# A hybrid decoder block on one core: the convolution norm in an early and a late part, and the first chunk's scores with the next four chunks'

## The chip, the core and the metric

The kernel runs on one core of one Trainium2 chip. The core has five engines that each work through their own queue of instructions in order: TensorE (PE, the matmuls, with PEld for its weight loads), VectorE (DVE), ScalarE (ACT), GpSimd (POOL) and SyncE (SP, which here only issues DMAs). They meet through semaphores. The metric is the device time of one execution in microseconds; lower is better.

## The reference

One decoder layer over 16 learned meta tokens and 512 tokens of 1024 channels, all in float32. Cut to what matters here:

```
p = layer_norm(concat(meta, x)) @ w_in          # one combined projection
c = p[:, :1024] * sigmoid(p[:, 1024:2048])      # conformer branch
c = causal_dwconv(c, 31 taps) + b
c = silu(layer_norm(c over channels, g, b)) @ w_conv_out
# RWKV-7 branch, 16 heads of 64, state S per head:
S_t = S_{t-1} diag(decay_t) + (S_{t-1} a_t) b_t^T + v_t k_t^T ;  y_t = S_t r_t
B = group_norm(y) ... @ w_rwkv_out
y = sigmoid(gA) * c + sigmoid(gB) * B
h = layer_norm(ALPHA*h + y @ w_o);  out = layer_norm(ALPHA*h + conv_gated_mlp(h))
```

## The kernel before

Channels lie on the 128 partitions, tokens along the free axis: 528 tokens in two halves of 272 and 256. Every large product is done in three matmuls per 128 channels of contraction (high part times high part, low times high, high times low), so a product of 128 output channels over one half of the tokens is a group of 24 matmuls into one PSUM bank. I call these groups the gemms. Their weights come by DMA (`wr`), ScalarE makes the high part (`wh`, L153) and VectorE the low part (`wl`, L154).

The eight PSUM banks are handed out by four rotating tags: three banks for `gbank` (all gemms of the first stage), two for `xbank` (the chain over chunks), two for `abank` and one for `mbank` (the preparation and small things).

The string SCHEDULE gives the program order of the first stage in steps, one letter and a pair of heads (0 to 7) each. G is `glu`, the conformer's gated product (four gemms). K is `rkv`, the projections k, v and r of a pair of heads (six gemms; r is last). P is `prep`, which turns them into the operands of the recurrence in 9 chunks of 64 tokens. S is `solve`, the triangular solves of a pair, a long run of small dependent VectorE operations, with the steps of a depthwise convolution `conv` of 48 VectorE operations put between them. C is `chain`, the recurrence from chunk to chunk. F is `finish`, A is `gate` (two gemms), T a convolution alone, N the norm of the convolutions, and H (before only) marks where gemms written later in the program are held behind the norm's mean. A priority scheduler then fixes each engine's queue: an instruction that is ready goes in order of its priority (program order, earlier inside `with front()`), and a tile from a rotating pool needs its place in the rotation.

`prep` in order, with the lines of before: two pairs of small products for decay and rate per half (L406, L407, L417, L418; row `ps_a<-lwp,wuh` and so on), tanh on ScalarE, squares summed per token (L454, `ps_m<-e,sq`), a scan on VectorE (L423, `cum`), exponentials, six products on VectorE that make the operands `AR` and `BK` (L434 to L448), the reciprocal norms (`nsc`, L456 to L460), their spread `nsb` transposed on TensorE (L468) and multiplied into `BK` (L470). Then come the bonus term `bv` (L478, L479), the scores of chunk 0, chunks 1 to 4 and chunks 5 to 8 (L490, each part of two heads into two `abank` banks, and L492 that masks them into `Gt`), a scaling of `AR` on ScalarE and transposes of `BK` and `v` (L506, L510).

`conv_norm` (N) loads the eight convolution results from `c_dr`, adds them (`csum`), forms the mean by a product with a matrix of ones (L802), subtracts it, squares on ScalarE and adds (`qsum`), forms the variance (L812), the root and its reciprocal, then scales, applies silu and splits into `zh`, `zl` for the product with `w_conv_out` (its first two weights at L182 to L184). It opens a pool of its own over the memory that the first stage leaves.

Of the kernel before, what the change touches and what calls it, by code (L numbers as in the profile page):

```python
# [11 lines left out]
F32 = mybir.dt.float32  # L12
F32R = mybir.dt.float32r
AF = mybir.ActivationFunctionType
ALU = mybir.AluOpType
# [3 lines left out]
P = 128  # L19
D = 1024  # L20
NK = D // P
SEQ = 512
NMETA = 16
T = SEQ + NMETA
HD = 64
NH = 16
NCH = 9
# [3 lines left out]
KC = 31  # L31
Q0 = 14
NQ = T - Q0
# [13 lines left out]
GW = 132  # L47


SCHEDULE = ("G0 K0 P0 T0 G1 S01 K1 P1 C0 K2 F0 G2 S12 K3 P2 C1 G3 F1 K4 S23 G4 P3 C2 F2 A S34 K5 P4 C3 F3 G5 S4 A "  # L50
            "T5 K6 P5 G6 C4 F4 S56 P6 C5 K7 F5 G7 S67 A A A P7 C6 F6 S7 A A C7 A A N A A A A H A A A F7")


@with_exitstack
def hybrid_block(ctx: ExitStack, tc: tile.TileContext, a, out, dbg=None):
    nc = tc.nc
    V, S, G, TE = nc.vector, nc.scalar, nc.gpsimd, nc.tensor
# [5 lines left out]
    def pool(stack, name, side, **kw):  # L63
        return stack.enter_context(tc.tile_pool(name=name, bufs=1, side=side, reuse_waits="tile", **kw))

    front = tc.high_priority
# [30 lines left out]
    ones_d = cp.tile([P, P], F32, name="ones_d")  # L97
# [9 lines left out]
    cmask = cp.tile([P, P], F32, name="cmask")  # L107
# [56 lines left out]
    def wload(dram, c0, wpool=None, bufs=2):  # L164
        return wsplit(wcols(dram, c0), [P, NK, P], wpool, bufs)

    hold = []

    def gemm(ps, w, xh, xl, sl, nk=NK):
        wh, wl = w  # L170
        for k in range(nk):
            first = TE.matmul(ps, wh[:, k, :], xh(k, sl), start=(k == 0), stop=False)  # L172
            if k == 0 and hold:
                behind(first, hold[-1], "work kept for the norm's waits")
            TE.matmul(ps, wl[:, k, :], xh(k, sl), start=False, stop=False)  # L175
            TE.matmul(ps, wh[:, k, :], xl(k, sl), start=False, stop=(k == nk - 1))  # L176

# [9 lines left out]
    turn, turn_a = cycle((gbank, xbank, gbank, xbank, gbank)), cycle((gbank, abank, gbank, abank, gbank))  # L187
# [21 lines left out]
    sp = pool(ctx_a2, "scan", "left")  # L209
    c_dr = dr.tile([NK, P, NQ], F32, name="c_dr")  # L210
# [38 lines left out]
    with tc.tile_pool(name="start", bufs=1, side="right", reuse_waits="tile") as st:  # L249
# [25 lines left out]
        for i, n in enumerate(names):  # L275
            src = a[n][0].rearrange("(r q) n -> r (q n)", q=2) if n == "r_k" else vec(n)
# [50 lines left out]
        for r_ in wr_:  # L327
            hi, lo, first = wparts(r_, [P, NK, P], wp)
# [9 lines left out]
        c0 = 43  # L338
        for i, n in ((1, 112), (2, 128), (3, 120), (4, 88), (5, 44)):
# [15 lines left out]
                    in1=taps[:, :, 1, :], op=ALU.add)  # L355
# [20 lines left out]
    ra = pool(ctx_a1, "proj", "right")  # L376
# [10 lines left out]
    def prep(p, r, k, v):  # L387
# [15 lines left out]
        for hf, (t0, t1) in enumerate(HALF):  # L403
            n = t1 - t0
# [3 lines left out]
            if hf == 0:  # L408
# [21 lines left out]
        AR = sp.tile([P, NCH, P], F32, name="AR", bufs=2)  # L430
        BK = ra.tile([P, NCH, P], F32, name="BK", bufs=1)
# [7 lines left out]
                               in1=Ei[:, :, 1:65], op0=ALU.mult, op1=ALU.mult)  # L439
        sq = ra.tile([P, 640], F32, name="sq", tag="tmp", bufs=2)[:, 0:OFF + T]  # L440
# [10 lines left out]
        pm = mbank()  # L451
# [12 lines left out]
        for g0, g1, c0, c1 in ((0, 3, 0, 5), (3, 5, 5, NCH)):  # L464
            pt = abank()
            for i in range(g0, g1):
# [4 lines left out]
                            in1=pt[:, 0:64 * (c1 - c0)].rearrange("p (c t) -> p c t", t=64), op=ALU.mult)  # L471


        bv = sp.tile([P, NQ], F32, name="bv", bufs=2)
        for t0, t1 in QH:
            pt = abank()
            n = t1 - t0
            TE.matmul(pt[:, :n], bones, rk[:, OFF + t0:OFF + t1], start=True, stop=True)  # L478
            V.tensor_tensor(out=bv[:, t0 - Q0:t1 - Q0], in0=pt[:, :n], in1=v[:, 64 + OFF + t0:64 + OFF + t1],  # L479
                            op=ALU.mult)  # L480


        Gt = sp.tile([P, 2, NCH, GW], F32, name="Gt", bufs=2)
        G.memset(Gt.rearrange("p h c (two x) -> p (h c two) x", two=2)[:, :, 64:66], 0.0)
        for c0, c1 in ((0, 1), (1, 5), (5, 9)):
            pts = [abank(), abank()]
            for c in range(c0, c1):
                for h in range(2):
                    o = pts[h][:, P * (c - c0):P * (c - c0 + 1)]
                    TE.matmul(o, BK[64 * h:64 * h + 64, c, :], AR[64 * h:64 * h + 64, c, :], start=True, stop=True)  # L490
            for h in range(2):
                V.tensor_tensor(out=Gt[:, h, c0:c1, :].rearrange("p c (two x) -> p c two x", two=2)[:, :, :, 0:64],  # L492
                                in0=pts[h][:, 0:P * (c1 - c0)].rearrange("p (c two t) -> p c two t", two=2, t=64),
                                in1=cmask.rearrange("p (two t) -> p two t", two=2).unsqueeze(1).broadcast_to(
                                    [P, c1 - c0, 2, 64]), op=ALU.mult)

        for c in range(1, NCH):
            S.activation(out=AR[:, c, :], in_=AR[:, c, :], func=AF.Copy, scale=lc[:, c - 1:c])
# [269 lines left out]
    def gate(j):  # L768
        w = wload(w_in, C_GA + P * j)
        gt = sp.tile([P, NQ], F32, name="gt", bufs=2)  # L770
        for t0, t1 in QH:
            pt = gbank()
            n = t1 - t0
            gemm(pt[:, :n], w, hh, hl, slice(t0, t1))
            with front():
                S.activation(out=gt[:, t0 - Q0:t1 - Q0], in_=pt[:, :n], func=AF.Tanh, scale=0.5,
                             bias=dcol(D_HBG, j))
        nc.sync.dma_start(out=g_dr[j], in_=gt)
# [3 lines left out]
    ctx_b1 = ExitStack()  # L782


    def conv_norm():
        rb = pool(ctx_b1, "conv", "right")
        zt = lambda dt, name: rb.tile([P, NQ], dt, name=name, tag="z", bufs=17)
        cs = []
        csum = rb.tile([P, NQ], F32, name="csum")
        for j in range(NK):  # L790
            c_t = zt(F32, "c_t")
            nc.sync.dma_start(out=c_t, in_=c_dr[j])
            cs.append(c_t)
            if j == 1:
                V.tensor_tensor(out=csum, in0=cs[0], in1=cs[1], op=ALU.add)
            elif j > 1:
                V.tensor_tensor(out=csum, in0=csum, in1=c_t, op=ALU.add)
        qsum = rb.tile([P, NQ], F32, name="qsum")
        rstd = rb.tile([P, NQ], F32, name="rstd")
        for sl, n in qsl:  # L800
            pm = abank()
            mean = TE.matmul(pm[:, :n], ones_d, csum[:, sl], start=True, stop=True)  # L802
            for j in range(NK):
                V.tensor_tensor(out=cs[j][:, sl], in0=cs[j][:, sl], in1=pm[:, :n], op=ALU.subtract)
        for j in range(NK):
            sq = qsum if j == 0 else zt(F32, "csq")
            S.activation(out=sq, in_=cs[j], func=AF.Square)
            if j > 0:
                V.tensor_tensor(out=qsum, in0=qsum, in1=sq, op=ALU.add)
        for sl, n in qsl:  # L810
            pm = abank()
            TE.matmul(pm[:, :n], ones_d, qsum[:, sl], start=True, stop=True)  # L812
            S.activation(out=rstd[:, sl], in_=pm[:, :n], func=AF.Sqrt, bias=eps_ln)
            V.reciprocal(out=rstd[:, sl], in_=rstd[:, sl])
        zh, zl = [], []
        for j in range(NK):
            V.tensor_tensor(out=cs[j], in0=cs[j], in1=rstd, op=ALU.mult)
            S.activation(out=cs[j], in_=cs[j], func=AF.Silu, scale=par("conv_ln_g", j), bias=par("conv_ln_b", j))
            zh.append(zt(F32R, "zh"))
            zl.append(zt(F32R, "zl"))  # L820
            split(zh[j], zl[j], cs[j])
        return rb, zh, zl, mean

    raw, prs, solved, ys, cpads = {}, {}, {}, {}, {}
    gates = list(range(16))
    for step in SCHEDULE.split():
        what, p, q = step[0], int(step[1:2] or 0), int(step[2:] or -1)
        if what == "K":
            raw[p] = rkv(p)
        elif what == "P":  # L830
            prs[p] = prep(p, *raw.pop(p))
        elif what == "S":
            solved[p] = solve(prs[p], conv(q, cpads.pop(q)) if q >= 0 else ())
        elif what == "C":
            with front():
                merge(prs[p], *solved[p])
                ys[p] = chain(prs[p])
        elif what == "F":
            finish(prs[p], ys.pop(p))
        elif what == "G":  # L840
            cpads[p] = glu(p)
        elif what == "T":
            with back():
                for _ in conv(p, cpads.pop(p)):
                    pass
        elif what == "A":
            gate(gates.pop(0))
        elif what == "N":
            ctx_a1.close()
            rb, zh, zl, mean = conv_norm()  # L850
        elif what == "H":
            hold.append(mean)
    hold.clear()
    for j in range(NK):
        ga = rb.tile([P, NQ], F32, name="ga", bufs=2)
        nc.sync.dma_start(out=ga, in_=g_dr[j])
# [23 lines left out]
    op = pool(ctx_o, "rout", "left")  # L880
# [119 lines left out]
    for j in range(2, NF):  # L1000
        c = j - 2
# [80 lines left out]
```

## Time and profile before

| | before |
|---|---|
| median of 3 runs | 1181.84 us (1171.94 to 1184.82) |
| profiled execution | 1175.08 us, its span 1173.0 us |
| TensorE busy | 1121.2 us, 96% of the span |
| VectorE busy | 862.9 us, 74% |
| ScalarE busy | 567.5 us, 48% |
| mean granted TensorE clock | 0.989 |

The busy time of TensorE is that of pipelined matmuls, so a full share does not say that it runs at its peak; its gaps are what is read here. The median of the runs is 0.6% above the profiled execution. The execution has 2.1 us around its span.

### The profile page before, as it was taken

To read this page: it belongs to the slowest core of one execution; us is meant where nothing else is said; L and a number is where in the kernel's file an instruction comes from. 1 tells how busy PE (TensorE), PEld (TensorE's weight loads), DVE (VectorE), ACT (ScalarE), POOL (GpSimd) and SP (SyncE) were. 2 spreads that over 40 slices of the span, in tenths; PEclk is the share of its full clock that TensorE was granted. 3 is DMA by queue.
4 is the path that set the end of the run, shared out by engine and by line. 5 is a ranking of instruction groups with operands and counts; after the bars stand their busy time and mean duration, and the time that the engine had idled before them with its cause. 6 is when DMAs were issued, how large, how long until landed. Compare 5 with 4: busy or idle time off the path is not lost.

```text
span 1173.0 us, 22681 instructions
## 1 busy us (share of the span) xinstructions
PE 1121.2 (96%) x8718; PEld 1056.2 (90%) x8718; DVE 862.9 (74%) x2179; ACT 567.5 (48%) x1214; POOL 83.6 (7%) x242
## 2 busy tenths in 40 slices
PE   5999999999999999999987999999999999999997
PEld 4998989899898989989887999998999999998885
DVE  6598998889899998976586366697876666662228
ACT  5644456637556565665577433355434343441120
POOL 7001011101101110101000000000000000000000
PEclk9999999999999999999988999999999999999999
DMA  5333341333414143354432476531332323333321
GB/s 163 84 93 92 87 97 50 87 77 91 101 56 109 42 103 79 85 125 106 140 100 65 139 227 203 158 88 54 109 109 73 108 73 109 89 123 113 102 78 72
DMA packets 202438, 118.99 MB, mean 101 GB/s; under 512 B 50036, under 2 KB 186397, under 8 KB 202331
## 3 DMA queue, kind: packets, MB, share of 16 engines
q1 hardware_dynamic: 182992, 113.81, 34.6%
q10 hardware_dynamic: 17515, 3.17, 1.5%
q8 instruction: 68, 1.11, 0.4%
q0 software_dynamic: 1824, 0.57, 0.3%
q14 instruction: 39, 0.32, 0.1%
HBM read 102.24 MB, written 15.28 MB: 100 GB/s over the span
## 4 chain that ended last, share of the span: by engine, by line
PE 65%; DVE 7%; DMA 4%; ACT 3%; issue 2%; DVEq 0%; ACTq 0%; POOL 0%; SPq 0%; POOLq 0%
PE ps_x L624 7%; PE ps_g L175 6%; PE ps_g L176 6%; PE ps_g L172 6%; PE ps_g L182 4%; PE ps_g L183 4%; PE ps_g L184 4%; PE psf L1027 3%; PE psf L1026 3%; PE psf L1028 3%; PE ps_x L182 3%; PE ps_x L183 3%; PE ps_x L184 3%; ACT wh L153 1%; PE ps_a L490 1%
## 5 line engine op out<-in xcount | busy, mean ns | idle before, releaser
L172 PE MATMUL ps_g<-hhi,wh 128*128 128x256 f32 (+2 forms) x944 | 278.9, 296 | 2.6 <-DVE v L227 1.7
L175 PE MATMUL ps_g<-hhi,wl 128*128 128x256 f32 (+2 forms) x944 | 278.6, 295 | 0.0
L176 PE MATMUL ps_g<-hlo,wh 128*128 128x256 f32 (+2 forms) x944 | 278.0, 295 | 0.0
L154 DVE TENSOR_TENSOR wl<-wr,wh 128x1024 fp32r<-128x1024 f32 x151 | 182.6, 1220 | 96.8 <-ACT wh L153 96.5
L153 ACT CAST wh<-wr 128x1024 fp32r<-128x1024 f32 x151 | 158.2, 1049 | 128.9 <-PE psf L1027 73.4
L172 PEld LDWEIGHTS ps_g<-hhi,wh 128*128 128x128 f32 x944 | 180.5, 191 | 5.2 <-DVE v L227 2.2
L175 PEld LDWEIGHTS ps_g<-hhi,wl 128*128 128x128 f32 x944 | 180.1, 191 | 2.6 <-issue 0.6
L176 PEld LDWEIGHTS ps_g<-hlo,wh 128*128 128x128 f32 x944 | 180.3, 191 | 1.4 <-issue 0.4
L182 PE MATMUL ps_g<-hhi,wh 128*128 128x256 f32 (+1 forms) x424 | 120.0, 283 | 0.0
L183 PE MATMUL ps_g<-hhi,wl 128*128 128x256 f32 (+1 forms) x424 | 119.2, 281 | 0.4 <-DVE wl L154 0.4
L184 PE MATMUL ps_g<-hlo,wh 128*128 128x256 f32 (+1 forms) x424 | 118.9, 281 | 0.0
L762 DVE SCALAR_TENSOR_TENSOR cev<-cd,drv,cev 128x257 f32<-128x257 f32 x216 | 99.1, 478 | 0.1
L182 PE MATMUL ps_x<-hhi,wh 128*128 128x256 f32 (+1 forms) x280 | 79.0, 282 | 1.7 <-ACT hhi L138 1.7
L183 PEld LDWEIGHTS ps_g<-hhi,wl 128*128 128x128 f32 x424 | 79.7, 188 | 0.7 <-DVE wl L154 0.7
L182 PEld LDWEIGHTS ps_g<-hhi,wh 128*128 128x128 f32 x424 | 79.7, 188 | 0.3 <-ACT wh L153 0.2
L184 PEld LDWEIGHTS ps_g<-hlo,wh 128*128 128x128 f32 x424 | 79.8, 188 | 0.0
L183 PE MATMUL ps_x<-hhi,wl 128*128 128x256 f32 (+1 forms) x280 | 78.6, 281 | 0.0
L184 PE MATMUL ps_x<-hlo,wh 128*128 128x256 f32 (+1 forms) x280 | 78.5, 280 | 0.0
L624 PE MATMUL ps_x<-UV,Gt 128*66 128x64 f32 (+1 forms) x576 | 70.7, 245 | 3.4 <-DMA Gt<-dT 2.6
L624 PEld LDWEIGHTS ps_x<-UV,Gt 128*66 128x66 f32 (+1 forms) x576 | 64.9, 166 | 5.1 <-DMA Gt<-dT 2.8
L1027 PE MATMUL psf<-wh,hidl 128*128 128x512 f32 x176 | 69.3, 394 | 0.0
L1026 PE MATMUL psf<-wh,hidh 128*128 128x512 f32 x176 | 69.0, 392 | 0.0
(371 smaller groups left out, 2542.6 us busy)
## 6 DMA issues: line engine op xcount, KB each, us to landing
wr<-in_w_in_dram SPq DMA_DIRECT2D x59, 512.0 KB, 4.3
wr<-in_ffn_up_dram SPq DMA_DIRECT2D x44, 512.0 KB, 4.0
wr<-in_ffn_down_dram SPq DMA_DIRECT2D x22, 512.0 KB, 3.6
wr<-in_w_o_dram SPq DMA_DIRECT2D x10, 512.0 KB, 4.9
g_dr<-gt SPq DMA_DIRECT2D x16, 257.0 KB, 2.9
L<-dA SPq DMA_DIRECT2D x32, 128.0 KB, 4.0
wr<-in_w_conv_out_dram SPq DMA_DIRECT2D x8, 512.0 KB, 4.3
wr<-in_w_rwkv_out_dram SPq DMA_DIRECT2D x8, 512.0 KB, 6.2
```

Of the source, the lines that this page charges most:

```text
L153: first = S.copy(out=hi, in_=raw)
L154: V.tensor_tensor(out=lo, in0=raw, in1=hi.bitcast(F32), op=ALU.subtract)
L172: first = TE.matmul(ps, wh[:, k, :], xh(k, sl), start=(k == 0), stop=False)
L175: TE.matmul(ps, wl[:, k, :], xh(k, sl), start=False, stop=False)
L176: TE.matmul(ps, wh[:, k, :], xl(k, sl), start=False, stop=(k == nk - 1))
L182: TE.matmul(ps, wh[:, k, :], xh(k, sl), start=(k == 0), stop=False)
L183: TE.matmul(ps, wl[:, k, :], xh(k, sl), start=False, stop=False)
L184: TE.matmul(ps, wh[:, k, :], xl(k, sl), start=False, stop=(k == nk - 1))
L624: mm = lambda o, l, r, start: TE.matmul(o, l, r, start=start, stop=True, skip_group_check=True)
L762: yield V.scalar_tensor_tensor(out=yp[:, b, :] if lasttap else ev[:, b, :], in0=d[:, i:i + NM], scalar=dcol(D_HCW, 8 * (2 * i + b) + j), i ...
L1026: TE.matmul(acc[t][d], hidh[:, k, ts], wd[k][0][:, ds], start=(k == 0), stop=False)
L1027: TE.matmul(acc[t][d], hidl[:, k, ts], wd[k][0][:, ds], start=False, stop=False)
```

## The change

Two edits. First, `prep` takes the banks of the first chunk's scores from `gbank` and `mbank` (two `abank` banks before), issues the scores of chunk 0 and of chunks 1 to 4 one behind the other at raised priority with the two heads in a fixed alternation, masks both parts after that, then does chunks 5 to 8; the bonus term `bv` moves behind the scores. Second, the norm is cut in two. A new step M, `conv_sums`, works in tiles of the convolutions' own memory (`cpad`, three buffers, `cacc`, `cev`): it loads the results one by one, adds them, takes the mean, loads them a second time, subtracts the mean, stores the centred values to a new `cc_dr`, squares and sums them and makes the reciprocal root. The late part N only loads `cc_dr`, scales, applies silu and splits. The step H and its `hold` go. In SCHEDULE, P7 moves ahead of the three gates that stood before it, and M stands behind P7.

```diff
-            "T5 K6 P5 G6 C4 F4 S56 P6 C5 K7 F5 G7 S67 A A A P7 C6 F6 S7 A A C7 A A N A A A A H A A A F7")
+            "T5 K6 P5 G6 C4 F4 S56 P6 C5 K7 F5 G7 S67 P7 M C6 A A A F6 S7 A A C7 A A N A A A A A A A F7")
...
-            if k == 0 and hold:
-                behind(first, hold[-1], "work kept for the norm's waits")
...
+        parts = ((0, 1), (1, 5), (5, 9))
+        score_banks = {}
+        for i, (c0, c1) in enumerate(parts):
+            pts = score_banks[i] = [gbank(), mbank()] if i == 0 else [abank(), abank()]
+            with front():
+                for c in range(c0, c1):
+                    for h in range(2):
+                        o = pts[h][:, P * (c - c0):P * (c - c0 + 1)]
+                        score = TE.matmul(o, BK[64 * h:64 * h + 64, c, :], AR[64 * h:64 * h + 64, c, :], start=True,
+                                          stop=True)
+                        if h == 0 and c > c0:
+                            behind(score, other, "the heads in turn")
+                        other = score
+            if i == 0:
+                continue
+            for i_, h in ((0, 0), (0, 1), (1, 0), (1, 1)) if i == 1 else ((2, 0), (2, 1)):
+                ... (the masking into Gt, as before)
...
-        for c0, c1 in ((0, 1), (1, 5), (5, 9)):
-            pts = [abank(), abank()]
-            for c in range(c0, c1):
-                for h in range(2):
-                    o = pts[h][:, P * (c - c0):P * (c - c0 + 1)]
-                    TE.matmul(o, BK[64 * h:64 * h + 64, c, :], AR[64 * h:64 * h + 64, c, :], start=True, stop=True)
...
+    def conv_tile(src=None):
+        c_t = ra.tile([P, 2, (KC - 1 + T) // 2], F32, name="cpad", bufs=3).rearrange("p two n -> p (two n)")[:, 0:NQ]
+        if src is not None:
+            nc.sync.dma_start(out=c_t, in_=src)
+        return c_t
+
+    def conv_sums():
+        csum = ra.tile([P, NQ], F32, name="cacc", bufs=1)
+        qsum = ra.tile([P, 2, NQ // 2], F32, name="cev", bufs=1).rearrange("p two n -> p (two n)")
+        for j in range(NK):
+            c_t = conv_tile(c_dr[j])
+            if j == 0:
+                c_0 = c_t
+            else:
+                V.tensor_tensor(out=csum, in0=c_0 if j == 1 else csum, in1=c_t, op=ALU.add)
+        for sl, n in qsl:
+            pm = abank()
+            TE.matmul(pm[:, :n], ones_d, csum[:, sl], start=True, stop=True)
+            S.copy(out=csum[:, sl], in_=pm[:, :n])
+        for j in range(NK):
+            c_t = conv_tile(c_dr[j])
+            V.tensor_tensor(out=c_t, in0=c_t, in1=csum, op=ALU.subtract)
+            nc.sync.dma_start(out=cc_dr[j], in_=c_t)
+            sq = qsum if j == 0 else conv_tile()
+            S.activation(out=sq, in_=c_t, func=AF.Square)
+            if j > 0:
+                V.tensor_tensor(out=qsum, in0=qsum, in1=sq, op=ALU.add)
+        rstd = sp.tile([P, NQ], F32, name="on", bufs=2)
...
+    def conv_norm(rstd):
+        rb = pool(ctx_b1, "conv", "right")
+        zt = lambda dt, name: rb.tile([P, NQ], dt, name=name, tag="z", bufs=17)
+        cs, zh, zl = [], [], []
         for j in range(NK):
+            cs.append(zt(F32, "c_t"))
+            nc.sync.dma_start(out=cs[j], in_=cc_dr[j])
...
+        elif what == "M":
+            rstd = conv_sums()
         elif what == "N":
             ctx_a1.close()
-            rb, zh, zl, mean = conv_norm()
-        elif what == "H":
-            hold.append(mean)
+            rb, zh, zl = conv_norm(rstd)
```

How this moves the queues, at three places. The first is TensorE's queue at the preparation of the last pair, from the transposes of `nsb` on. Rows `ps_g<-hhi` and `ps_g<-hlo` are gemms, `ps_x` rows are the chain of the pair before. Before:

```order
L468 MATMUL ps_a<-ident,nsb 128x66
L175 MATMUL ps_g<-hhi,wl 128x256
L176 MATMUL ps_g<-hlo,wh 128x256
L624 MATMUL ps_x<-Sb_567,AR 128x128
L624 MATMUL ps_x<-UV,Gt 66x64 x2
L468 MATMUL ps_a<-ident,nsb 128x128 x4
L172 MATMUL ps_g<-hhi,wh 128x258
L175 MATMUL ps_g<-hhi,wl 128x258
L176 MATMUL ps_g<-hlo,wh 128x258
```

Of the change, at the same pair (L402 to L414 are the small products, L464 the transposes, L482 the scores, L615 the first product of the solves' merge):

```order
L402 MATMUL ps_a<-lwp,wuh 128x256
L403 MATMUL ps_a<-lwp,wul_555 128x256
L413 MATMUL ps_a<-lap,wuh 128x256
L414 MATMUL ps_a<-lap,wul_555 128x256
L464 MATMUL ps_a<-ident,nsb 128x66
L464 MATMUL ps_a<-ident,nsb 128x128 x4
L482 MATMUL ps_g<-AR,BK 128x128
L482 MATMUL ps_a<-AR,BK 128x128
L482 MATMUL ps_m<-AR,BK 128x128
L482 MATMUL ps_a<-AR,BK 128x128 x7
L615 MATMUL ps_m<-t11n,a_561 128x32 x4
L170 MATMUL ps_g<-hhi,wh 128x258
```

The gemms and chain rows that stood among the preparation's products are gone from between them; the next gemm stands behind the scores.

The second place is VectorE's queue of the change at the same pair, from the evacuation of the last gemm that TensorE has ahead of that preparation (L745, into `cpad`): L573 and L575 are steps of the solve of pair 6, L763 steps of convolution 7.

```order
L745 SCALAR_TENSOR_TENSOR cpad<-cpad,ps_g 128x2x128
L760 TENSOR_TENSOR cd_6635<-cpad 128x272
L573 TENSOR_TENSOR stmp<-L,W 128x63
L761 TENSOR_TENSOR cd_6636<-cpad 128x271
L154 TENSOR_TENSOR wl<-wr,wh 128x1024
L575 TENSOR_TENSOR W<-W,stmp 128x3x21
L763 SCALAR_TENSOR_TENSOR csh<-cpad,drv,csh 128x257
...
L771 SCALAR_TENSOR_TENSOR cacc<-cd_6635,drv,cev 128x257
L419 SCALAR_TENSOR_TENSOR cum<-smask,E 128x585
L433 SCALAR_TENSOR_TENSOR BK<-th,k 128x9x64
L452 TENSOR_SCALAR nsc<-ps_m 66x2
```

Before, in the same queue, the convolution's last steps also end ahead of the scan, with the chain's `Sb` among the preparation:

```order
L762 SCALAR_TENSOR_TENSOR cacc<-cd_6634,drv,cev 128x257
L456 TENSOR_SCALAR nsc<-ps_m 66x2
L457 TENSOR_SCALAR nsc<-ps_m 128x8
L459 RECIPROCAL nsc<-nsc 66x2
L460 RECIPROCAL nsc<-nsc 128x8
L437 SCALAR_TENSOR_TENSOR BK<-th,k 128x9x64
L655 SCALAR_TENSOR_TENSOR Sb_568<-Sb_567,lc,ps_x 64x64 x2
L423 SCALAR_TENSOR_TENSOR cum<-smask,E 128x585
```

What moved is what TensorE has beside these rows: before it has gemms of gates and the chain, in the change nothing until the scan and the products behind it are done.

The third place is TensorE's queue at the mean. Before, the two products stand at the end of a chain:

```order
L624 MATMUL ps_x<-Rz_565,Gt 66x64 x2
L624 MATMUL ps_x<-UV,Gt 128x64 x2
L802 MATMUL ps_a<-csum,ones_d 128x258
L802 MATMUL ps_a<-csum,ones_d 128x256
L172 MATMUL ps_g<-hhi,wh 128x258
```

Of the change, they stand among the chain's first steps of pair 6, several hundred rows ahead of the first product that reads `zh`:

```order
L519 MATMUL ps_a<-ident,v 128x128 x3
L815 MATMUL ps_a<-cacc,ones_d 128x258
L633 MATMUL ps_x<-UV,BT 128x128
L633 MATMUL ps_x<-UV,Gt 128x64 x2
L815 MATMUL ps_a<-cacc,ones_d 128x256
```

What moved is the distance: from the variance to the first product with `zh` there were 34 gemm matmuls before, there are 500 rows now.

## Rows read from the trace of the kernel before

**Rows 1.** The page: span, and part 1, busy time by engine.
```profile
span 1173.0 us, 22681 instructions
PE 1121.2 (96%) x8718; PEld 1056.2 (90%) x8718; DVE 862.9 (74%) x2179; ACT 567.5 (48%) x1214; POOL 83.6 (7%) x242
```

**Rows 2.** Windows: us, busy PE, PEld, DVE, ACT, POOL (counts), clock, DMA, GB/s.
```profile
87.00:561.00 474.00, 461.79 (x3795) 431.93 (x3795) 415.97 (x1341) 274.33 (x673) 55.94 (x154) 0.99 0.35 86
```

**Rows 3.** Waits of PE: line, waited for, us in total, times, longest.
```profile
PE ps_g L182 <- ACT zh L138: 6.9, 1, 6.9
...
PE ps_a L802 <- DVE csum L797: 3.5, 1, 3.5
...
PE ps_a L812 <- DVE qsum L809: 0.4, 1, 0.4
...
PE ps_a L510 <- DVE Gt L492: 0.4, 1, 0.4
```

**Rows 4.** Windows of PE alone: us, busy, granted clock, DMA share, GB/s.
```profile
583.00:590.40 7.40, 2.65 (x23) 0.84 0.44 141
590.40:594.40 4.00, 4.00 (x14) 0.50 0.20 72
...
622.58:625.60 3.02, 3.02 (x14) 0.50 0.47 142
```

**Rows 5.** Timeline of PE at the preparation of pair 0: start us, us, what.
```profile
71.91 0.28 PE L406 MATMUL ps_a<-lwp,wuh 128*128 128x272 f32 x1
72.03 0.29 PE L407 MATMUL ps_a<-lwp,wul 128*128 128x272 f32 x1
...
72.40 1.12 PE L454 MATMUL ps_m<-e,sq 128*66 128x2 f32 x10
...
83.25 0.60 PE L468 MATMUL ps_a<-ident,nsb 128*128 128x128 f32 x4
```

**Rows 6.** Timeline of DVE at the same preparation.
```profile
77.34 1.64 DVE L423 TENSOR_TENSOR_SCAN cum<-smask,E 128x585 f32<-128x585 f32 x1
78.90 0.46 DVE L762 SCALAR_TENSOR_TENSOR cev<-cd,drv,cev 128x257 f32<-128x257 f32 x1
...
82.15 1.22 DVE L154 TENSOR_TENSOR wl<-wr,wh 128x1024 fp32r<-128x1024 f32 x1
83.29 0.81 DVE L446 SCALAR_TENSOR_TENSOR rk<-r,prm,BK 128x576 f32<-128x576 f32 x1
84.02 0.43 DVE L736 SCALAR_TENSOR_TENSOR cpad<-cpad,ps_g 128x272 f32<-128x272 f32 x1
84.36 0.75 DVE L448 TENSOR_TENSOR BK<-BK,Ei 128x576 f32<-128x576 f32 x1
85.03 0.81 DVE L470 TENSOR_TENSOR BK<-BK,ps_a 128x320 f32<-128x320 f32 x2
```

**Rows 7.** Timeline of DVE: solve and convolution steps in turn.
```profile
259.14 0.48 DVE L762 SCALAR_TENSOR_TENSOR cev<-cd,drv,cev 128x257 f32<-128x257 f32 x1
...
259.66 0.48 DVE L762 SCALAR_TENSOR_TENSOR cev<-cd,drv,cev 128x257 f32<-128x257 f32 x1
```

**Rows 8.** Timeline of DVE: convolution steps alone, and solve steps alone.
```profile
245.05 2.48 DVE L762 SCALAR_TENSOR_TENSOR cev<-cd,drv,cev 128x257 f32<-128x257 f32 x6
...
614.79 0.21 DVE L566 TENSOR_TENSOR W<-W,stmp 128x48 f32<-128x48 f32 x1
615.03 0.21 DVE L564 TENSOR_TENSOR stmp<-L,W 128x49 f32<-128x49 f32 x1
```

**Rows 9.** Instructions of L492: count, ns shortest/median/longest, first and last start.
```profile
L492 DVE TENSOR_TENSOR Gt<-ps_a,cmask x48: 279/682/693, 87.5 to 562.1; 128x512 f32<-128x512 f32 x32, 128x128 f32<-128x128 f32 x16
```

**Rows 10.** DMA issues: queue, count, KB each, median us to landing.
```profile
c_t<-c_dr SPq DMA_DIRECT2D x8, 257.0 KB, 4.9
...
dT<-W SPq DMA_DIRECT2D x16, 32.0 KB, 2.0
...
t<-dT SPq DMA_DIRECT2D x8, 64.0 KB, 3.6
```

More of the change, by code (lines that the diff above doesn't have):

```diff
@@ L165, in wload @@
         return wsplit(wcols(dram, c0), [P, NK, P], wpool, bufs)
-    hold = []
     def gemm(ps, w, xh, xl, sl, nk=NK):
@@ L171, in gemm @@
         for k in range(nk):
-            first = TE.matmul(ps, wh[:, k, :], xh(k, sl), start=(k == 0), stop=False)
-            if k == 0 and hold:
-                behind(first, hold[-1], "work kept for the norm's waits")
+            TE.matmul(ps, wh[:, k, :], xh(k, sl), start=(k == 0), stop=False)
             TE.matmul(ps, wl[:, k, :], xh(k, sl), start=False, stop=False)
@@ L471, in prep @@
                             in1=pt[:, 0:64 * (c1 - c0)].rearrange("p (c t) -> p c t", t=64), op=ALU.mult)
+        Gt = sp.tile([P, 2, NCH, GW], F32, name="Gt", bufs=2)
+        G.memset(Gt.rearrange("p h c (two x) -> p (h c two) x", two=2)[:, :, 64:66], 0.0)
+        parts = ((0, 1), (1, 5), (5, 9))
[14 more added lines that the diff above has]
+            for i_, h in ((0, 0), (0, 1), (1, 0), (1, 1)) if i == 1 else ((2, 0), (2, 1)):
+                c0, c1 = parts[i_]
+                pts = score_banks[i_]
+                V.tensor_tensor(out=Gt[:, h, c0:c1, :].rearrange("p c (two x) -> p c two x", two=2)[:, :, :, 0:64],
+                                in0=pts[h][:, 0:P * (c1 - c0)].rearrange("p (c two t) -> p c two t", two=2, t=64),
+                                in1=cmask.rearrange("p (two t) -> p two t", two=2).unsqueeze(1).broadcast_to(
+                                    [P, c1 - c0, 2, 64]), op=ALU.mult)
         bv = sp.tile([P, NQ], F32, name="bv", bufs=2)
@@ L480, in prep @@
                             op=ALU.mult)
-        Gt = sp.tile([P, 2, NCH, GW], F32, name="Gt", bufs=2)
-        G.memset(Gt.rearrange("p h c (two x) -> p (h c two) x", two=2)[:, :, 64:66], 0.0)
-        for c0, c1 in ((0, 1), (1, 5), (5, 9)):
-            pts = [abank(), abank()]
-            for c in range(c0, c1):
-                for h in range(2):
-                    o = pts[h][:, P * (c - c0):P * (c - c0 + 1)]
-                    TE.matmul(o, BK[64 * h:64 * h + 64, c, :], AR[64 * h:64 * h + 64, c, :], start=True, stop=True)
[L491 to L495, printed above, removed]
         for c in range(1, NCH):
@@ L782, in hybrid_block @@
     ctx_b1 = ExitStack()
[L785 to L789, printed above, removed]
-        for j in range(NK):
[L791 to L799, printed above, removed]
+    cc_dr = dr.tile([NK, P, NQ], F32, name="cc_dr")
+    def conv_tile(src=None):
[6 more added lines that the diff above has]
+        qsum = ra.tile([P, 2, NQ // 2], F32, name="cev", bufs=1).rearrange("p two n -> p (two n)")
+        for j in range(NK):
+            c_t = conv_tile(c_dr[j])
[3 more added lines that the diff above has]
+                V.tensor_tensor(out=csum, in0=c_0 if j == 1 else csum, in1=c_t, op=ALU.add)
         for sl, n in qsl:
             pm = abank()
-            mean = TE.matmul(pm[:, :n], ones_d, csum[:, sl], start=True, stop=True)
-            for j in range(NK):
-                V.tensor_tensor(out=cs[j][:, sl], in0=cs[j][:, sl], in1=pm[:, :n], op=ALU.subtract)
+            TE.matmul(pm[:, :n], ones_d, csum[:, sl], start=True, stop=True)
+            S.copy(out=csum[:, sl], in_=pm[:, :n])
         for j in range(NK):
-            sq = qsum if j == 0 else zt(F32, "csq")
-            S.activation(out=sq, in_=cs[j], func=AF.Square)
+            c_t = conv_tile(c_dr[j])
[3 more added lines that the diff above has]
+            S.activation(out=sq, in_=c_t, func=AF.Square)
             if j > 0:
                 V.tensor_tensor(out=qsum, in0=qsum, in1=sq, op=ALU.add)
+        rstd = sp.tile([P, NQ], F32, name="on", bufs=2)
         for sl, n in qsl:
@@ L814, in conv_norm @@
             V.reciprocal(out=rstd[:, sl], in_=rstd[:, sl])
-        zh, zl = [], []
+        return rstd
+    def conv_norm(rstd):
[5 more added lines that the diff above has]
+            nc.sync.dma_start(out=cs[j], in_=cc_dr[j])
         for j in range(NK):
@@ L821, in conv_norm @@
             split(zh[j], zl[j], cs[j])
-        return rb, zh, zl, mean
+        return rb, zh, zl
     raw, prs, solved, ys, cpads = {}, {}, {}, {}, {}
@@ L847, in hybrid_block @@
             gate(gates.pop(0))
+        elif what == "M":
+            rstd = conv_sums()
         elif what == "N":
             ctx_a1.close()
-            rb, zh, zl, mean = conv_norm()
-        elif what == "H":
-            hold.append(mean)
-    hold.clear()
+            rb, zh, zl = conv_norm(rstd)
     for j in range(NK):
```

## The prediction

> **What bounds the kernel now.** I read the shares of the engines first. TensorE is busy 1121.2 of 1173.0 us [rows 1], so at most 52 us of the whole span are its gaps, and a change can win much only by taking instructions from it, which this one does not. The window from the first preparation to the end of the last one says more: in 474 us TensorE is busy 461.8 and VectorE 416.0 [rows 2], that is 97% and 88%. TensorE paces the stage, and VectorE is close behind it: it has few holes in which a backlog could vanish. The waits of TensorE come next. The two that the norm causes are the longest behind the program's start that one cause explains: 3.5 us for the sum and 6.9 us for the first `zh`, while masking of scores costs it 0.4 us once [rows 3]. The windows around them show a second price: from 583.0 to 590.4 us TensorE is idle 7.40 - 2.65 = 4.75 us, and in the next 4.0 us it runs at a granted clock of 0.50 (of 2.4 GHz, so 1.2); behind the 6.9 us it runs 3.0 us at 0.50 [rows 4]. Half speed for 4.0 and 3.0 us loses 2.0 and 1.5.
>
> **What the norm's split gives.** The idle times before the mean, variance and `zh` go: 4.75 + 0.4 + 6.9, and the half clock with them, 2.0 + 1.5 [rows 3, 4]. Together 15.6 us. In exchange come eight more loads, eight stores, eight loads of `cc_dr`, two copies on ScalarE, and fewer subtractions on VectorE (8 of 514 columns, 16 halves before). They lie beside the gates and the chain: between variance and first `zh` product TensorE has 500 rows, some 60 us at 0.12 each [rows 5], against 34 rows before. If that cover were gone, at most the 15.6 us would return. One thing I charge: M's first loads wait for `cpad` buffers and its sum stands in VectorE's queue ahead of work that pair 7's scores need; one load, 4.9 us [rows 10].
>
> **What the scores' edit does to TensorE's queue.** This is the large term, and it is not in the diff's words but in the order of the queues. Before, between the first of the small products of a preparation and its first score TensorE had 87, 279, 154, 130, 246, 218, 259 and 222 gemm matmuls for pairs 0 to 7. In the change it has none, in any pair; only pair 4 has 6 and pair 6 has 19 other rows there. A likely reason (the queue shows the fact, not the reason): the first score now takes its bank from the same rotation of three as the gemms, and a later gemm's bank is handed out only behind it. TensorE works in order, so it stands through whatever lies between the small products and the second `BK`.
>
> How long is that? With nothing ahead of it, from the small products to the scan 77.34 - 71.91 = 5.4 us [rows 5, 6]. From the scan to the end of the second `BK` 85.84 - 77.34 = 8.5, in which VectorE also does a weight's low part (1.14 start to start), one evacuation (0.34) and one convolution step (0.4); without these 6.6 [rows 6]. In pairs 1, 2, 3 and 7 the four `nsc` operations and the copy of `nsb` come behind the scan too; I add 1.5, an estimate from four solve steps of 0.24 [rows 8] and half a us for the copy. TensorE's own work inside is 8 x 0.12 + 1.12 + 0.6 = 2.7 [rows 5].
>
> VectorE's queue has more ahead of the scan: all steps of convolution and solve that stand between the evacuation of TensorE's last gemm and the scan. VectorE can't begin them before that gemm ends, so TensorE stands for them too. Prices, start to start: a convolution step and a solve step together 259.66 - 259.14 = 0.52 [rows 7]; a convolution step alone 2.48 / 6 = 0.41, a solve step alone 615.03 - 614.79 = 0.24 [rows 8]; the evacuation about 0.5. TensorE's idle time is then the larger of 5.4 and this backlog, plus 6.6 or 8.1, less 2.7:
> - pairs 0 and 5 (3 and 2 convolution steps): 5.4 + 6.6 - 2.7 = 9.3 each
> - pair 1 (24 convolution, 25 solve): 0.5 + 24 x 0.52 + 0.24 + 1.14 = 14.4, + 8.1 - 2.7, and 10 solve steps inside (2.4): 22.2
> - pair 2 (25 and 19): 14.0 + 8.1 - 2.7 = 19.4
> - pair 3 (13 and 8, three convolution steps inside, 1.2): 7.9 + 8.1 - 2.7 + 1.2 = 14.5
> - pair 4 (16 solve): 5.5 + 6.6 - 2.7, less six rows at 0.12: 8.7
> - pair 6 (48 and 42, seven small ones): 27.6 + 6.6 - 2.7, less 19 rows: 29.2
> - pair 7 (48 and 42, two additions of M inside, 0.8): 25.9 + 8.1 - 2.7 + 0.8 = 32.1
>
> Sum 144.7 us. None of it lies beside other work of TensorE, since nothing else stands there.
>
> **Smaller terms.** Pair 1's merge stands close behind: a write of 2.0 and a read of 3.6 us follow the solve's end [rows 10], 5.6. Behind the scores of seven pairs the chain's first steps wait for the masks, two of 0.28 and two of 0.68 us ahead of what they need [rows 9], 1.9 each, say 2.0: 14 (0 where gemms cover it, 4 if VectorE is late once more). The clock: two idle times of 4.75 and 6.9 us cost 2.0 and 1.5 [rows 3, 4], so eight of 9 to 32 us cost about 1.8 each, 14.4. What `bv` loses by its place is hidden behind the masks; fixed turns of the heads and the different banks cost TensorE no row more.
>
> **Sum.** 1175.1 - 15.6 + 144.7 + 4.9 + 5.6 + 14 + 14.4 = 1343 us against the profiled execution. The median of the runs before is 0.6% above that execution, so for the median of the runs 1350.
>
> The first gap in the profile's stage is one for each pair. The Trainium skill (Perfetto Trace Analysis, Optimization Strategy) says that the same gap repeating on the engine that should be saturated can mean that the next tile couldn't be allocated. No row before shows such a gap; the order of the change, by the bank that it takes, would be a case of it.
>
> **Rivals.**
> 1. *Faster.* The order costs nothing, because VectorE and not TensorE sets the pace: idle time in front of the scores only replaces later waits, and the norm's gain stays: 1175.1 - 15.6 = 1159.5. For it: VectorE's 88% [rows 2]. Against it: TensorE has almost no waits there to replace, 474 - 461.8 = 12.2 us in all [rows 2]. It decides if a stall costs under 15.6 / 8 = 2 us; even pair 0's bare chain takes 9.3. The Trainium skill (Perfetto Trace Analysis, Matmuls) wants independent groups of matmuls to rotate through different PSUM banks, so that evacuation lies beside the next group; by that the edit could only win, since scores of chunks 0 and 1 to 4 no longer share two banks. The trace has 0.4 us for that wait [rows 3], so it would win next to nothing. Chance 0.02.
> 2. *Only the bare chains.* VectorE does its backlog earlier than I think, in time that it had over: 8 x 9.3 + 14.4 - 15.6 + 1175.1 = 1248, with the smaller terms 1273. Against it: the evacuation stands ahead of the steps in the same queue, in order. Chance 0.07.
> 3. *More.* Backlog returns behind each stall: gemms restart and wait for evacuations behind masks, six preparation products and the solve. Another 10 us a pair, as long as a bare chain, gives 1423. For it: VectorE's 88% [rows 2]. Against it: in the stalls VectorE gets ahead. Chance 0.08.
> 4. *The norm's second pass is not covered.* Sixteen loads and eight stores through three buffers, 16 x 4.9 / 3 = 26 us [rows 10], partly ahead of the products: up to 1369, inside the range. Chance 0.03.
>
> **How the numbers follow.** The forecast has 0.80. Its own lower end: no smaller terms (-24.5), half the clock's loss (-7), the four small operations hidden (-6), the small products' chain 1.5 shorter in pairs 0 and 5 (-3), VectorE five steps ahead of its queue in pairs 1, 2, 6 and 7 (5 x 0.52 each, -10): 1292. Its upper end: durations in place of pitches, 0.69 for 0.52 in 135 pairs of steps (+23) [rows 7, 8], the smaller terms twice (+24.5), the clock twice (+14): 1405. For the median of the runs, 0.6% more, 1300 to 1412; cases 2 and 3 are left out with 0.15, and case 4 lies inside. About 1% is what a measurement of this kernel can tell from no change; only case 1 lies below it: faster 0.02, same 0.02 (a case 1 in which the norm's gain goes too), slower 0.96.
>
> **What would show it.** In the profile after: TensorE waits for `nsb` at L464 and for `BK` at the first score L482 in every pair, in sum per pair about 30 us for pairs 6 and 7, 20 for 1 and 2, 9 for 0, 4 and 5; a granted clock of 0.50 behind each; between these rows no gemm; no wait for `zh` at L178, and none over 1 us at L815 and L828. VectorE in these gaps is busy with L763, L573 and L575, not idle. It is wrong if TensorE's idle time in the first stage is under 100 us, if gaps of pairs 6 and 7 are not three times those of pairs 0 and 5, or if gemms are found inside.

## The result and the profile after

The changed kernel takes 1324.6 us in the median of its runs (1320.7 to 1331.4), 1.122 times the kernel before (95% interval 1.117 to 1.126). The forecast was 1350, range 1300 to 1412. The profiled execution took 1325.9 us, its span 1324.0, against 1175.1 and 1173.0 before; the sum of the prediction for it was 1343.

The page after, parts 1 and 2 (busy tenths in 40 slices, and the granted clock of TensorE):

```profile
PE 1150.6 (87%) x8718; PEld 1079.4 (82%) x8718; DVE 882.3 (67%) x2171; ACT 577.0 (44%) x1218; POOL 83.5 (6%) x242
...
PE   5979399498797978397298999999899999999997
...
PEclk9969699599696979589599999999999999999999
```

TensorE runs the same 8718 matmuls [rows 1]. It is idle for 1324.0 - 1150.6 = 173.4 us, 121.6 more than before, and busy 29.4 us longer with the same work. The two make the whole difference of the spans, 151.0. The holes in the row of PE, each with a low clock beside or behind it, come in the first half, one for each pair of heads.

What TensorE waited for (line, waited for, us in total, times, longest):

```profile
PE ps_a L464 <- ACT nsb L458: 117.9, 8, 29.2
PE ps_g L482 <- DVE BK L466: 7.7, 8, 2.3
...
PE ps_x L695 <- ACT Y L691: 6.2, 4, 4.7
...
PE ps_a L402 <- ACT E L407: 3.4, 6, 0.9
...
PE ps_a L828 <- DVE cev L824: 0.9, 1, 0.9
```

Eight times `nsb`, eight times `BK`: the two places that the prediction named. The waits for `zh` and for the sum [rows 3] are gone, that for the variance (`cev` at L828) is 0.9. The timeline of TensorE's waiting rows (start, us, what, and in brackets the idle time before it) shows the stalls of pairs 0, 1, 5, 6 and 7 (the row of 529.28 is the finish of an earlier pair, inside pair 6's stall):

```profile
74.21 0.39 PE L402 MATMUL ps_a<-lwp,wuh 128*128 128x256 f32 x1 [0.59 <-ACT E L407]
...
80.36 1.63 PE L464 MATMUL ps_a<-ident,nsb 66*128 66x66 f32 x5 [5.27 <-ACT nsb L458]
84.30 0.58 PE L482 MATMUL ps_g<-AR,BK 64*128 64x128 f32 x1 [2.31 <-DVE BK L466]
...
153.84 1.63 PE L464 MATMUL ps_a<-ident,nsb 66*128 66x66 f32 x5 [22.39 <-ACT nsb L458]
...
481.21 1.63 PE L464 MATMUL ps_a<-ident,nsb 66*128 66x66 f32 x5 [5.41 <-ACT nsb L458]
485.16 0.58 PE L482 MATMUL ps_g<-AR,BK 64*128 64x128 f32 x1 [2.31 <-DVE BK L466]
...
529.28 0.47 PE L695 MATMUL ps_x<-ident,Y 128*128 128x128 f32 x1 [4.72 <-ACT Y L691]
...
557.85 1.63 PE L464 MATMUL ps_a<-ident,nsb 66*128 66x66 f32 x5 [18.92 <-ACT nsb L458]
...
651.59 1.63 PE L464 MATMUL ps_a<-ident,nsb 66*128 66x66 f32 x5 [29.18 <-ACT nsb L458]
```

What VectorE does while TensorE stands for pair 7, from its timeline (the evacuation of the last gemm, the first steps, the last ones, the scan):

```profile
619.26 0.42 DVE L745 SCALAR_TENSOR_TENSOR cpad<-cpad,ps_g 128x256 f32<-128x256 f32 x1 [2.36 <-PE ps_g L172]
...
621.83 0.48 DVE L763 SCALAR_TENSOR_TENSOR csh<-cpad,drv,csh 128x257 f32<-128x257 f32 x1
622.23 0.21 DVE L573 TENSOR_TENSOR stmp<-L,W 128x60 f32<-128x60 f32 x1
622.36 0.48 DVE L763 SCALAR_TENSOR_TENSOR csh<-cpad,drv,csh 128x257 f32<-128x257 f32 x1
...
644.18 0.91 DVE L771 SCALAR_TENSOR_TENSOR cacc<-cd,drv,cev 128x257 f32<-128x257 f32 x2
644.97 1.40 DVE L419 TENSOR_TENSOR_SCAN cum<-smask,E 128x585 f32<-128x585 f32 x1
```

VectorE is not idle. From the evacuation (619.26) to the scan (644.97) it works 25.7 us through convolution and solve; the prediction had 25.9. A pair of steps takes 622.36 - 621.83 = 0.53, as in [rows 7].

Pair by pair, TensorE's idle time from the first small product to the first score (the waits at L402, L464 and L482, and those of the rows of chain and finish that stand between them: 0.9 for pair 4, 6.3 for pair 6) against the terms of the prediction, in us:

| pair | 0 | 1 | 2 | 3 | 4 | 5 | 6 | 7 | sum |
|---|---|---|---|---|---|---|---|---|---|
| predicted | 9.3 | 22.2 | 19.4 | 14.5 | 8.7 | 9.3 | 29.2 | 32.1 | 144.7 |
| measured | 8.2 | 23.1 | 18.9 | 13.3 | 8.6 | 8.3 | 25.4 | 30.5 | 136.3 |

The clock is the larger surprise. Windows of TensorE alone, behind the stalls of pair 0, of pair 1 and, at its end, of pair 7 (us, busy, granted clock, DMA share, GB/s):

```profile
84.30:88.30 4.00, 4.00 (x27) 0.50 0.02 5
88.30:92.30 4.00, 4.00 (x22) 0.50 0.03 8
92.30:96.30 4.00, 4.00 (x17) 0.50 0.32 51
96.30:100.30 4.00, 4.00 (x29) 0.94 0.09 31
155.60:159.60 4.00, 3.97 (x32) 0.68 0.44 68
159.60:163.60 4.00, 4.00 (x36) 1.00 0.12 23
...
663.70:665.70 2.00, 2.00 (x9) 0.50 0.43 70
665.70:667.70 2.00, 2.00 (x13) 0.73 0.23 36
```

Behind pair 0's stall of 8.2 us TensorE is busy without a gap and yet at 0.50 for over 12 us. Behind the norm's idle times before it was about 4.0 and 3.0 [rows 4]. The rows next behind the stalls are where the busy time grew: the same 288 products of the scores took 49.7 us in place of 33.2, the same 64 of the merge of the solves 15.1 in place of 9.0. Four of these at a granted clock of 1.00 (behind pair 1) and four at 0.50 (behind pair 3), both of the changed kernel:

```profile
160.00 0.62 PE L620 MATMUL ps_m<-t,pp 128*32 128x128 f32 x4
...
347.56 1.06 PE L620 MATMUL ps_m<-t,pp 128*32 128x128 f32 x4
```

### The profile page after: what moved, and what is told of

It is laid out like the page before. It is cut to its first block, busy times and chain, and to the rows that moved or that the text cites. A ratio compares the mean times of both kernels' runs of the same rounds, so it can differ in the third digit from the quotient of the medians.

```text
span 1324.0 us, 22741 instructions
## 1 busy us (share of the span) xinstructions
PE 1150.6 (87%) x8718; PEld 1079.4 (82%) x8718; DVE 882.3 (67%) x2171; ACT 577.0 (44%) x1218; POOL 83.5 (6%) x242
## 4 chain that ended last, share of the span: by engine, by line
PE 70%; DVE 20%; DMA 5%; ACT 3%; issue 2%; ACTq 0%; SPq 0%; DVEq 0%
PE ps_g L170 8%; PE ps_x L633 8%; PE ps_g L171 8%; PE ps_g L172 8%; DVE cev L771 5%; PE ps_g L178 4%; PE ps_g L179 4%; PE ps_g L180 4%; PE psf L1050 3%; PE psf L1049 3%; PE ps_x L178 3%; PE psf L1051 3%; PE ps_a L482 3%; PE ps_x L179 3%; PE ps_x L180 3%; DVE csh L763 2%
## 5 line engine op out<-in xcount | busy, mean ns | idle before, releaser
L464 PE MATMUL ps_a<-ident,nsb 128*128 128x128 f32 (+1 forms) x40 | 11.9, 420 | 119.1 <-ACT nsb L458 117.9
L464 PEld LDWEIGHTS ps_a<-ident,nsb 128*128 128x128 f32 (+1 forms) x40 | 7.2, 209 | 122.5 <-ACT nsb L458 119.8
```

## The experiments

Twelve kernels, each timed against the kernel before on the same chip (its median there 1177.9 to 1178.8); the ratio that stands behind each time is to that. Three theories stand against each other. The bank: chunk 0's scores in the gemms' rotation keep every later gemm behind them. The early issue: raised priority, fixed turns and late masking do it. The norm: its cut, its second loads or the moved preparation cost the time.

**The bank alone, in the kernel before.**

```diff
-            pts = [abank(), abank()]
+            pts = [gbank(), mbank()] if c0 == 0 else [abank(), abank()]
```

> The kernel before, with one edit: the first chunk's scores take a bank of the gemms' rotation and the small one, in place of the two `abank` banks; masked at once, normal priority, old norm, old order of steps. Theory 1 (the bank alone takes the gemms out of the preparation): 0 gemm matmuls between the small products and the scores in all pairs, TensorE waits about 100 to 130 us in sum for `nsb` and `BK`, pair 7 less than in the change (three gates stand ahead of its small products, 144 gemms at 0.12 = 17 us in which VectorE works), a half clock behind each stall: 1320 us, 1300 to 1345. Theory 2 (early issue and raised priority take them out, not the bank): within 5 us of before, 1175 to 1187.

Measured: 1323.4 us, 1.1205 (1.1128 to 1.1282). TensorE's waits:

```profile
PE ps_a L468 <- ACT nsb L462: 113.2, 8, 24.6
...
PE ps_a L478 <- DVE BK L470: 5.5, 8, 2.3
```

One line in the kernel before gives a loss as large as the whole change's. In its trace, too, TensorE has no gemm between the small products and the scores of any pair.

**The scores' edit without the norm's.**

> The change's edit of the scores alone, with the old norm and the old order of steps. Theory 1 (the bank): like the kernel before with the bank alone, within 8 us of it; so 1300 to 1345, and TensorE's waits for `zh` and the sum (6.9 and 3.5 us) are back. If early issue and alternation cost or give anything of their own, it is the distance to the kernel with the bank alone. Theory 3 (the norm's cut and the moved preparation of pair 7 are what costs): within 10 us of before.

Measured: 1306.9 us, 1.1082 (1.1028 to 1.1135). The waits for `nsb` are 105.7, for `BK` 7.3. So the rest of the scores' edit does not cost; the kernel is 16 us shorter than the one with the bank alone, where a distance under 8 was expected. Unexpected: the waits for the sum and for `zh` of [rows 3], which this old norm should still have, are not among TensorE's waits.

**The norm's cut without the scores' edit.**

> The change's norm in two parts and its order of steps alone, with the old scores. Theory 1: the norm gains its 15.6 us (idle 12.1, half clock 3.5) and nothing of the stalls appears: 1165 us, 1158 to 1172. Rival: the second loads and stores make TensorE wait at the mean and variance, or pair 7's preparation ahead of the gates lengthens the end: 1181 to 1200. Theory 3 (the norm's cut is what costs): over 1250.

Measured: 1183.1 us, 1.0035 (1.0012 to 1.0058). No stall, and no gain either: the forecast's 15.6 us are not there. TensorE's waits, and windows of TensorE alone (us, busy, granted clock, DMA share, GB/s):

```profile
PE ps_a L815 <- DVE cev L811: 5.1, 1, 5.1
...
PE ps_x L704 <- ACT on L698: 4.5, 1, 4.5
```

```profile
600.00:610.00 10.00, 8.60 (x69) 1.00 0.74 199
610.00:620.00 10.00, 2.70 (x9) 0.68 0.70 196
620.00:630.00 10.00, 6.99 (x32) 0.50 0.77 192
```

L815 is the variance in this kernel, L704 a product of a finish. The wait moved from the mean and `zh` to the variance, with 7.3 us idle in one window and the half clock behind it. That is the prediction's rival 4, in the small.

**The whole change with another bank.** Two versions: one bank of the chain's rotation, or the two `abank` banks of before, masked before the next part's scores.

```diff
-            pts = score_banks[i] = [gbank(), mbank()] if i == 0 else [abank(), abank()]
+            pts = score_banks[i] = [xbank(), mbank()] if i == 0 else [abank(), abank()]
```

> The whole change, but the first chunk's scores take a bank of the chain's rotation of two in place of one of the gemms' three. Theory 1: the gemms stand among the preparation again (84 to 280 in the queue for a pair), no wait above 3 us for `nsb` or `BK`, clock near 0.98: 1160 to 1180, the norm's gain less what the chain loses by one bank. Theory 2 (early issue at raised priority): still over 1290.

> The whole change, but the first chunk's scores take the two `abank` banks as before and are masked before the next four chunks' scores; raised priority, fixed turns and the late bonus term stay. Theory of the bank: no stall above 3 us in the preparations, 1158 to 1172, about as the norm's cut alone. If raised priority or the late bonus term cost: above the norm's cut alone by over 10 us.

Measured: 1170.2 us, 0.9925 (0.9898 to 0.9952) with `xbank`; 1169.2, 0.9922 (0.9896 to 0.9949) with `abank`. In the second one the first page row is `PE 1118.7 (96%)`, and the window in which the change had its stall of pair 1 reads (TensorE alone):

```profile
140.00:165.00 25.00, 23.71 (x186) 1.00 0.42 103
```

The same scores at the same priority, in the `xbank` version also the same late masking and the same `mbank`, and 154 us less. Both are 0.8% below the kernel before. With this the cause is shown from both sides: add the bank to the kernel before, or take it from the change. Not tried was a fourth bank for the gemms (all eight are handed out), so that it is the turn in the rotation, and not that the gemms have two free banks left of three, is argued and not shown.

**Without raised priority.**

> The whole change without raised priority for the scores; their bank still comes from the gemms' rotation. Theory 1 (the bank): still no gemm in the preparations, waits for `nsb` and `BK` of 110 to 135 us in sum, 1310 to 1340. Theory 2 (raised priority): under 1200.

Measured in one run: 1346.3 us, a little above what was expected, with waits for `nsb` of 121.7 and for `BK` of 7.9.

```profile
PE 1167.5 (87%) x8718; PEld 1091.5 (81%) x8718; DVE 881.0 (66%) x2171; ACT 576.3 (43%) x1218; POOL 84.4 (6%) x242
```

Priority does not make the stalls. Against the change this run is some 20 us longer, and 17 of them are TensorE's busy time (1167.5 against 1150.6), not its waits; a single run does not show more than that.

**Is a stall VectorE's backlog, or the chain's own latency?** First the three gates ahead of pair 7's preparation again (`S67 A A A P7 M C6 F6 S7`), which gives VectorE three gates' time to start on the same steps.

> The whole change, but the three gates stand ahead of pair 7's preparation again (the sums of the norm behind it, as in the change). No gemm comes between the small products and the scores of any pair, and VectorE has the same 48 convolution and 42 solve steps ahead of the scan of pair 7; but they can begin three gates earlier: 144 gemms at 0.12 = 17 us. If TensorE's stall is that backlog: pair 7's wait falls from 29.7 to about 12 us, and the time to about 1305 (1300 to 1312). If the stall were the serial chain's own latency: unchanged, 1320 to 1330.

Measured: 1309.1 us, 1.1101 (1.1048 to 1.1154), 14 to 15 less than the change (by the ratios and by the medians). Pair 7's wait:

```profile
654.71 1.63 PE L464 MATMUL ps_a<-ident,nsb 66*128 66x66 f32 x5 [15.80 <-ACT nsb L458]
```

From 29.2 to 15.8, with the wait for `BK` 16.3 in all, where about 12 was expected. This also says why the bank alone, in the old order of steps, cost as much as the whole change: the rest of the scores' edit saves about 16 us and the moved preparation of pair 7 costs 14 to 15, so that the two losses agree by chance. Then the other way, again with no gemm between the small products and the scores: everything from the scan to the second `BK` `with front():`, so that VectorE has few steps ahead of the scan.

> The whole change, with the preparation from the scan to the second `BK` at raised priority, so that VectorE has 3 to 14 steps of convolution and solve ahead of the scan in place of up to 90; TensorE still has no gemm there. If pairs 1, 2, 3, 6 and 7 stand for VectorE's backlog: every stall falls to the bare chain, about 8 us, 8 x 8 = 64 in place of 134, so TensorE's waits for `nsb` and `BK` fall to 50 to 75 us in sum, and the time to 1255 (1240 to 1275, some of the backlog may come back at the merges). If the stalls are latency of the chain: over 1300.

Measured: 1265.3 us, 1.0724 (1.0674 to 1.0774).

```profile
PE 1155.2 (91%) x8718; PEld 1082.0 (86%) x8718; DVE 875.1 (69%) x2171; ACT 571.3 (45%) x1216; POOL 89.9 (7%) x242
```

```profile
PE ps_a L465 <- ACT nsb L459: 32.6, 8, 4.9
PE ps_g L483 <- DVE BK L467: 18.8, 7, 3.2
PE ps_a L402 <- ACT E L407: 8.8, 5, 3.0
```

The waits at these three lines fall from 129.0 to 60.2, where 64 was expected: about half of the stalls was backlog, the rest is the bare chain of eight preparations. Yet TensorE is busy 1155.2, a little more than in the change: stalls half as long cost as much clock.

**The same priority where gemms cover.**

> The norm's cut with the old scores, and the preparation from the scan to the second `BK` at raised priority. TensorE has gemms beside the preparation (154 to 312 a pair), so nothing waits for the scan: if cover is all that matters, the time stays within 5 us of the norm's cut alone (about 1165). If VectorE's order costs also with cover, it is faster by 5 us or more; if the convolutions that come later hold the norm's sums back, slower.

Measured: 1196.6 us, 1.0147 (1.0090 to 1.0203), so 13 us slower than the norm's cut alone, and not within 5 us of it as cover alone would have it. From 60 to 540 us TensorE does 139 matmuls fewer than there (3726 against 3865) and is busy 7 us less (461.57 against 468.89), and the wait for the variance is 5.8 (5.1 there). Which of the postponed steps it is that the rest then waits for was not settled.

**Where do the 9 us of the two faster versions come from?** Three kernels around the `abank` version.

> The scores with `abank` banks, raised priority, fixed turns and the late bonus term, with the old norm and the old order of steps. The whole change with these scores took 1169.2, the norm's cut alone 1183.1, before 1178.4. If the cut of the norm gives what was gained and the scores only let it (they bring the chain, and with it the sums, earlier): 1175 to 1182. If the scores themselves give the 9 us and the cut nothing: 1165 to 1172.

> The whole change with `abank` banks for the scores (1169.2), and the bonus term ahead of the scores again. It differs from the norm's cut alone (1183.1) by raised priority and fixed turns only. If the late bonus term gives the 14 us between them (two products and two VectorE operations fewer ahead of the chain): 1180 to 1186. If raised priority gives it: 1165 to 1173.

> The whole change with `abank` banks for the scores (1169.2) and the three gates ahead of pair 7's preparation. With gemms among the preparation nothing stands for VectorE's backlog, so the place of the gates should cost less than it did in the change (15 us there): within 5 us of 1169. If the norm's sums or the end of pair 7's chain are late by it, the wait for the variance comes back: 1175 to 1185.

Measured: with the old norm and order 1170.7, 0.9939 (0.9914 to 0.9965); with the bonus term ahead of the scores 1182.6, 1.0046 (1.0025 to 1.0067); with the gates ahead of pair 7's preparation 1171.0, 0.9931 (0.9910 to 0.9952). So the late bonus term gives the gain (1182.6 to 1169.2), raised priority and fixed turns nothing that can be measured under cover (1182.6 against 1183.1), the norm's cut nothing (1169.2 against 1170.7, the intervals overlap), and the place of pair 7 nothing once gemms stand beside it. The instructions of the masking (count, shortest, median and longest ns, first and last start), of the `abank` version, of the same with the old norm and order, and of the bonus term first:

```profile
L490 DVE TENSOR_TENSOR Gt<-ps_a,cmask x48: 281/682/693, 86.5 to 537.4; 128x512 f32<-128x512 f32 x32, 128x128 f32<-128x128 f32 x16
```

```profile
L494 DVE TENSOR_TENSOR Gt<-ps_a,cmask x48: 279/682/693, 86.4 to 539.3; 128x512 f32<-128x512 f32 x32, 128x128 f32<-128x128 f32 x16
```

```profile
L498 DVE TENSOR_TENSOR Gt<-ps_a,cmask x48: 283/681/693, 88.4 to 565.6; 128x512 f32<-128x512 f32 x32, 128x128 f32<-128x128 f32 x16
```

With the bonus term last the last mask starts at 537.4 in place of 565.6. With the old norm and order it starts at 539.3, and in the kernel before it was 562.1 [rows 9]: pair 7's masks come 23 us earlier than before, and of the old norm's waits for the sum and for `zh` none is left among TensorE's waits. The bonus term alone was not moved in the kernel before, and whether it delays the scores by its operations or by the two `abank` banks that it takes ahead of them was not tried.

## Why the prediction was right, and where its terms were wrong

Right were the place, the way and the size. The step that carried it was the reading of TensorE's queue: no gemm between the small products and the scores. That a bank of the gemms' rotation is the reason was marked as likely; the bank alone in the kernel before (1323.4) and the change without it (1169.2, 1170.2) show it. By the Trainium skill (Perfetto Trace Analysis, Optimization Strategy) the same gap repeating on the engine that should be saturated can mean that there is no room for the next tile: the trace has such gaps, eight and 117.9 us at one line, and the runs put them down to a bank, though there were as many banks as before.

The stalls were 136.3 for 144.7. Prices and counts held: 25.7 for 25.9 us of backlog at pair 7, 0.53 for 0.52 a pair of steps, and taking the backlog away left 60 us. The error is small and nearly all of one sign. A part of it is that TensorE's own work inside a stall runs at the half clock: the transposes at L464 take 1.63 us (row of 80.36) where I had 0.60 of the full clock [rows 5], so that a microsecond more of each stall is busy time. And in pairs 4 and 6 the trace has 12 and 29 matmuls of chain and finish there, where I had counted 6 and 19.

Three terms were mis-sized:
- The smaller terms, 4.9 + 5.6 + 14 = 24.5, came to nothing. The idle time grew by 121.6: the stalls' 136.3 less the norm's 12.1 leaves -2.6 for all the rest. The first steps of the chain wait 0.2 to 0.7 us behind a stall, not 2, and pair 1's merge hardly: VectorE, as I read it, gets ahead while TensorE stands. That was the argument against rival 3 (another 10 us a pair), which falls with them, and I did not hold it against my own extras.
- The clock, 14.4, was too small. TensorE is busy 29.4 us longer; the norm's own half clock of 3.5 should have gone, so the stalls' is about 33. I took 1.8 a stall from two idle times of the kernel before; behind these stalls the half clock lasts up to 13 us of busy time (the rows up to 667.70). My price of half the time comes out too high in turn: the time at 0.50 behind the eight stalls is some 83 us, which it would put at 42, and the merge's products lose 0.44 of 1.06 us, not half.
- The norm's -15.6 was no gain of the norm's cut. Without stalls the cut alone is 0.35% slower, with `abank` scores it makes no difference, and with stalls it makes none either (1.1101 against 1.1082, pair 7 behind the gates in both). The step that failed is "the idle times before the mean, variance and `zh` go". In the change they do go, but with the old norm they go as well (the kernels of 1306.9 and 1170.7), and with the cut alone the wait moves to the variance. In the sum over the change the figure still stood at the right place, since these waits were gone beside the stalls.

The errors have different signs: +18.5 for the clock, -8.4 for the stalls, about 0 for the norm in this sum, and -27.1 for the smaller terms, which are what is left of the difference. Together they are the 17 us from 1343 to the profiled 1325.9, while two of them are 27 and 19 with opposite signs: a part of the closeness is luck. Another 7 us of the distance from 1350 to 1324.6 are the 0.6% that I added for the median of the runs; of the changed kernel the profiled execution is not shorter than the median.

Also wrong: that the late bonus term gains and loses nothing. It is worth 13 us with the cut norm, and with raised priority and the old norm 7 against the kernel before. I looked only at what it hides behind and not at what it stands ahead of: its two products and two VectorE operations came between `BK` and the scores.

Of the rivals, the first falls: TensorE sets the pace. The second, bare chains only, is the kernel with the scan at raised priority: 1265.3, where I had 1248 to 1273. The Trainium skill (Perfetto Trace Analysis, Matmuls) wants independent groups of matmuls to rotate through different PSUM banks so that they overlap with evacuation; my reading of it, by which the edit could only win, was too wide: the scores did get other banks, and what decided was whose rotation they came from.

## What to carry to other kernels

A bank taken from a rotation orders its users. In this kernel the tile that waited for a long serial chain came from the rotation of the work that covered this chain, and the cover was gone; it should come from another. Read that from the queue of the engine that paces, by counting what it has between the start of the chain and its first user, before any duration is looked at. A stall of an engine that works in order is then not the chain's latency alone, but also what the other engine's queue holds ahead of the chain. And work that the next step doesn't need, as the bonus term here, belongs behind that step.

## What the runs showed of the hardware that was not expected

The half clock behind an idle time does not scale with it. Behind pair 0's stall of 8.2 us TensorE ran at a granted clock of 0.50 (1.2 GHz) for over 12 us of unbroken busy time, behind pair 7's of 30.5 us for about 13, behind pair 1's of 23.1 us for about 3, and behind the norm's idle times of 4.75 and 6.9 us before for about 4.0 and 3.0 [rows 4]. With the stalls cut from 129 to 60 us in sum the engine's busy time was 1155.2 in place of 1150.6. What makes pair 1 recover sooner was not tried: in the first 4 us behind its stall TensorE has 32 matmuls, behind pair 0's 27, 22 and 17 in 4 us each.
